# Phase tables of the S5 chunks made on GpSimd instead of VectorE

## The chip, the cores and the metric

The kernel runs on one core of one Trainium2 chip. The metric is the device time of one execution in microseconds (us), the median of three runs: 1687.13 us before the change (1683.44 to 1687.8).

## The reference, cut to what matters

One decoder layer is computed for 1024 prompt tokens and 32 sample tokens (8 sequences of 4), 1056 columns in all. A combined projection `h @ w_in` gives queries, keys, values, the S5 input `u` and gate logits. Branch A is windowed attention. Branch B, the one that matters here, is a diagonal complex recurrence per group of 16 channels (64 groups, 64 states each):

```
dt = exp(log_dt);  decay = exp(lam_re * dt)
ab_re, ab_im = decay * cos(lam_im * dt), decay * sin(lam_im * dt)     # A_bar
h_t = A_bar * h_(t-1) + B_bar * u_t                                   # scan over positions
y_t = Re(C h_t) + D * u_t
```

Then gelu, a GLU projection, a gated merge of both branches, the output projection, RMSNorm, a squared-ReLU MLP and a final RMSNorm.

## The kernel before, in words

All matrix products run in split precision: each float32 factor is cut into a high part (`whi`, cast on ScalarE, L91) and a low part (`wlo`, subtraction on VectorE, L92), and TensorE makes three products of them (L117 to L119). `w_in` is loaded in blocks of 128 columns; `tile_in` (L505) multiplies one block with all 1056 tokens in three chunks of 352. Three PSUM banks (`mm`) take the chunks in turn, so a bank must be emptied before the third chunk after it begins. For a block of `u`, VectorE empties the bank into `Up` (L435, L440, L441); for a block of gates, ScalarE or VectorE copies it into `gt` (L493, L495), which a DMA takes away.

The S5 branch is worked in eight tiles m of eight groups. The positions are cut into 128 chunks of eight tokens. The scan over chunks is made real by taking the rotation of A_bar out: for that the kernel needs the cosine and sine of the phase of every chunk number k from 0 to 127. They come about in steps:

- `s5_params` (L266 on, VectorE) makes dt, the decay, cosine and sine, the powers of A_bar in `TP`, and then, in a chain of nine doublings of eight small instructions each (L374 to L381, 128x32), the phases of the chunk numbers 1, 2, 4, ..., 64. The last seven go into the tile `TE`.
- `s5_phases` (L404) builds from `TE` two small tables `AB`: 16 low and 8 high parts of the chunk number, cosine and sine. It begins with four memsets (L410, L411) and then doubles the tables in seven steps of six products or sums (L420 to L425), of 32, 64, 128 and 256 elements for the low part and 32, 64 and 128 for the high part. Each step needs the step before it (save that the high part begins anew) and one entry of `TE`.
- Two DMAs of the SyncE queue write `AB` to DRAM (L427), and for each tile m a DMA reads its part back as `ab` (L605).
- `s5_e` (L599 on) multiplies low and high parts out to the full tables `EC` and `ES` of tile m (L619 to L621 on VectorE, L625 and L626 on ScalarE), and `s5_x` uses them (first at L652).

GpSimd has little to do in this stretch: per tile m two products of `s5_a` (L555 and L567), whose results VectorE then adds (L556, L568).

The order of the instructions on each engine and each DMA queue is not the order of the lines. A planner in the framework runs through the program once when it is built, with its own estimate of each instruction's time and with the order of the lines as priority, and writes down one fixed order for each engine. On the chip each engine goes through its own list in that order and waits where an input or a buffer is not ready. So the phase steps stand interleaved with the chain L374 to L381 and with other work of VectorE. The buffers `AB[0]`, `AB[1]` and the work tile `aw` lie in a pool of 20 slabs, 16 of which hold the split activations; they come free from tiles of `s5_loads` and `s5_tables` (the last one, for `aw`, after L403).

Of the kernel before, what the change touches and what calls it, by code (L numbers as in the profile page):

```python
# [45 lines left out]
def hybrid_kernel(tc, xt, cache_k, cache_v, h0, norms, w_in, sinks, w_attn_o, lam_re, lam_im, log_dt,  # L46
                  b_ri, b_ir, c_ri, d_cols, w_glu, w_out, w_up, w_down, w_last,
                  y_cols, y_rows, k_prompt, v_prompt, ssm_prompt, k_sample, v_sample, ssm_sample, dbg=None):
    nc = tc.nc
    uid = [0]  # L50

    def new(pool, shape, dt, tag, bufs=None):
        uid[0] += 1
        return pool.tile(list(shape), dt, tag=tag, name=f"{tag}_{uid[0]}", bufs=bufs)
# [211 lines left out]
    def s5_params(pt, lr, li, ldt):  # L266

        V = nc.vector

        def small(tag, w=G, dt=F32):  # L270
            return new(pt, [P, w], dt, tag)

        def exp(out, x, w):
            k, r, p, xc = small(f"ek{w}", w), small(f"er{w}", w), small(f"ep{w}", w), small(f"ex{w}", w)
            i = small(f"ei{w}", w, I32)
            V.tensor_scalar(xc, x, -87.0, 88.0, op0=ALU.max, op1=ALU.min)
            V.tensor_scalar(k, xc, LOG2E, MAGIC, op0=ALU.mult, op1=ALU.add)
            V.tensor_scalar(k, k, -MAGIC, None, op0=ALU.add)
            V.scalar_tensor_tensor(r, k, -LN2_HI, xc, op0=ALU.mult, op1=ALU.add)
            V.scalar_tensor_tensor(r, k, -LN2_LO, r, op0=ALU.mult, op1=ALU.add)  # L280
            V.tensor_scalar(i, k, 8388608.0, 127 * 8388608.0, op0=ALU.mult, op1=ALU.add)
# [122 lines left out]
    def s5_phases(TE):  # L404

        AB = [new(slabA, [P, KT, 24, 4], F32, "slab") for _ in range(2)]
        aw = new(slabA, [P, KT, 2, 8, 4], F32, "slab")
        V = nc.vector
        for o in (0, 16):
            V.memset(AB[0][:, :, o:o + 1], 1.0)  # L410
            V.memset(AB[1][:, :, o:o + 1], 0.0)  # L411
        for i in range(7):
            o, h = (0, 1 << i) if i < 4 else (16, 1 << (i - 4))
            sh = [P, KT, h, 4]
            cb = TE[:, i][:, :, None, :].to_broadcast(sh)
            sb = TE[:, 7 + i][:, :, None, :].to_broadcast(sh)
            x, y = AB[0][:, :, o:o + h], AB[1][:, :, o:o + h]
            zc, zs = AB[0][:, :, o + h:o + 2 * h], AB[1][:, :, o + h:o + 2 * h]
            w1, w2 = aw[:, :, 0, 0:h], aw[:, :, 1, 0:h]
            V.tensor_tensor(zc, x, cb, op=ALU.mult)  # L420
            V.tensor_tensor(w1, y, sb, op=ALU.mult)
            V.tensor_tensor(zs, y, cb, op=ALU.mult)
            V.tensor_tensor(w2, x, sb, op=ALU.mult)
            V.tensor_tensor(zc, zc, w1, op=ALU.subtract)
            V.tensor_tensor(zs, zs, w2, op=ALU.add)  # L425
        for i in range(2):
            nc.sync.dma_start(abdram[:, i], AB[i])  # L427
# [267 lines left out]
    tile_in()  # L695
    us = [s5_u(0)]
    s5_phases(ft[2])
    w2 = s5_a(0)
    tile_in()
# [532 lines left out]
    V = nc.vector  # L1232
# [430 lines left out]
```

## Time and profile before

| | |
|---|---|
| median of the runs | 1687.13 us (1683.44 to 1687.8) |
| the profiled execution, own time | 1690.28 us |
| its span, first to last instruction | 1688.6 us |
| TensorE matmul busy | 1647.2 us, 98% of the span |
| VectorE busy | 1227.5 us, 73% |
| ScalarE busy | 874.6 us, 52% |
| GpSimd busy | 246.6 us, 15%, 229 instructions |
| mean granted TensorE clock | 0.991 of full speed |

The profile comes from one execution. Engines are PE (TensorE matmul), PEld (its weight load), DVE (VectorE), ACT (ScalarE), POOL (GpSimd) and SP (SyncE); a name such as SPq is the engine's queue, which issues DMAs. Times in a timeline count from the start of the span. What an instruction waited for stands in square brackets behind its row: the idle time of its engine, and what ended it. A duration in a timeline includes the time in which an instruction that has been issued waits for a port.

### The profile page before, as it was taken

The page shows a single profiled execution, that of the slowest core. Times are in us where ns is not written, and L with a number is a line of the kernel's source. Part 1 is how long each engine was busy: PE and PEld are TensorE (multiplying, and loading weights), DVE is VectorE, ACT ScalarE, POOL GpSimd, SP SyncE. Part 2 cuts the span into 40 slices and gives each one's busy share as a digit, 9 for nine tenths or more (in the row PEclk, how much of TensorE's full clock was granted, in tenths as well). Part 3 has the DMA queues.
Part 4 walks back from the last instruction along what each step waited for, and adds up shares of the span by engine and source line. Part 5 has one row for each costly group of instructions (what it writes and reads, how often), then busy time and mean ns, then how long its engine had stood idle before and what let it go on. Part 6 is the DMA issues. An engine that isn't in the chain of part 4 may idle for free. (4 is left out here: it accounts for less than half of the span.)

```text
span 1688.6 us, 30936 instructions
## 1 busy us (share of the span) xinstructions
PE 1647.2 (98%) x11976; PEld 1613.3 (96%) x11976; DVE 1227.5 (73%) x2460; ACT 874.6 (52%) x1889; POOL 246.6 (15%) x229
## 2 busy tenths in 40 slices
PE   9999999999999999989999999999999999999998
PEld 8989899999999898989999999999999999999987
DVE  7977888753489999842644677777777788787866
ACT  6234454434567788643433655444444645454544
POOL 1102111101233344320222330000000000000010
PEclk9999999999999999988999999999999999999999
DMA  6334344435502211232343553444444665353422
GB/s 246 113 115 130 106 124 141 136 107 164 206 26 89 78 52 64 84 119 89 123 146 128 187 168 115 153 151 151 150 145 147 224 203 180 109 180 118 123 63 104
DMA packets 133992, 221.84 MB, mean 131 GB/s; under 512 B 14012, under 2 KB 86796, under 8 KB 133332
## 3 DMA queue, kind: packets, MB, share of 16 engines
q1 hardware_dynamic: 86756, 170.81, 31.6%
q10 hardware_dynamic: 45360, 46.63, 8.2%
q0 software_dynamic: 1728, 2.41, 0.5%
q8 instruction: 94, 1.54, 0.4%
q14 instruction: 54, 0.44, 0.1%
HBM read 150.58 MB, written 69.22 MB: 130 GB/s over the span
## 5 line engine op out<-in xcount | busy, mean ns | idle before, releaser
L117 PE MATMUL mm<-slab,whi 128*128 128x352 f32 (+3 forms) x1688 | 535.9, 320 | 8.6 <-DVE Up L440 3.3
L118 PE MATMUL mm<-slab,whi 128*128 128x352 f32 (+3 forms) x1688 | 530.4, 314 | 1.9 <-DVE slab L994 1.9
L119 PE MATMUL mm<-slab,wlo 128*128 128x352 f32 (+3 forms) x1688 | 530.7, 315 | 0.3 <-DVE wlo L92 0.3
L1248 PE MATMUL ax<-slab,w 128*128 128x264 f32 x3600 | 451.6, 285 | 1.8 <-DVE acc L1323 1.8
L1248 PEld LDWEIGHTS ax<-slab,w 128*128 128x128 f32 x3600 | 443.8, 188 | 3.0 <-DVE acc L1323 2.7
L117 PEld LDWEIGHTS mm<-slab,whi 128*128 128x128 f32 x1688 | 320.1, 190 | 12.8 <-PE mm L119 4.4
L118 PEld LDWEIGHTS mm<-slab,whi 128*128 128x128 f32 x1688 | 321.6, 191 | 4.0 <-DVE slab L994 3.3
L119 PEld LDWEIGHTS mm<-slab,wlo 128*128 128x128 f32 x1688 | 320.4, 190 | 1.0 <-DVE wlo L92 0.6
L1248 PE MATMUL mm<-slab,w 128*128 128x264 f32 x1440 | 186.7, 284 | 1.8 <-DVE w L1359 1.1
L1248 PEld LDWEIGHTS mm<-slab,w 128*128 128x128 f32 x1440 | 179.8, 188 | 2.5 <-DVE w L1359 1.3
L91 ACT CAST whi<-raw 128x1024 fp32r<-128x1024 f32 x76 | 79.7, 1049 | 90.2 <-PE mm L118 64.7
L1359 DVE TENSOR_TENSOR w<-raw,w 128x512 fp32r<-128x512 f32 (+2 forms) x96 | 63.0, 657 | 77.1 <-ACT w L1358 73.3
L92 DVE TENSOR_TENSOR wlo<-raw,whi 128x1024 fp32r<-128x1024 f32 x76 | 97.5, 1283 | 22.4 <-ACT whi L91 22.2
L1560 POOL TENSOR_TENSOR slab<-slab,slab 128x512 f32<-128x512 f32 x7 | 9.1, 1294 | 633.1 <-ACT slab L1557 633.1
L1358 ACT CAST w<-whi 128x512 fp32r<-128x512 f32 (+2 forms) x64 | 38.0, 594 | 70.1 <-PE ax L1248 43.4
L839 ACT ACTIVATE pm<-pm,sm 128x128 f32<-128x128 f32 x128 | 49.9, 391 | 34.1 <-DVE sm L836 34.0
L815 POOL TENSOR_TENSOR qs<-q,qs 64x256 fp32r<-64x256 f32 x64 | 58.1, 907 | 63.7 <-ACT qs L814 32.3
L1272 ACT ACTIVATE slab<-slab 128x264 f32<-128x264 f32 x80 | 33.9, 425 | 59.8 <-DVE slab L1271 44.1
L1358 ACT CAST w<-raw 128x512 fp32r<-128x512 f32 (+2 forms) x96 | 56.8, 593 | 9.6 <-PE mm L1248 7.9
L854 POOL TENSOR_TENSOR pt<-fb,pt 128x512 fp32r<-128x512 f32 x28 | 41.7, 1488 | 123.4 <-ACT pt L853 80.1
L567 POOL TENSOR_TENSOR tmp<-bbs,TP 128x1024 f32<-128x1024 f32 x8 | 23.2, 2897 | 209.6 <-DVE W L556 172.9
L1359 DVE TENSOR_TENSOR w<-wlo,w 128x512 fp32r<-128x512 f32 (+2 forms) x64 | 42.1, 658 | 4.8 <-ACT w L1358 3.7
(407 smaller groups left out, 2661.4 us busy)
## 6 DMA issues: line engine op xcount, KB each, us to landing
raw<-in_w_in_dram SPq DMA_DIRECT2D x36, 512.0 KB
raw<-in_w_up_dram SPq DMA_DIRECT2D x32, 512.0 KB
ffd<-slab ACTq DMA_DIRECT2D x28, 528.0 KB
gt<-ffd SPq DMA_DIRECT2D x53, 264.0 KB
slab<-ffd SPq DMA_DIRECT2D x53, 264.0 KB
raw<-in_w_down_dram SPq DMA_DIRECT2D x22, 512.0 KB
gd<-gt ACTq DMA_DIRECT2D x48, 176.0 KB
slab<-gd SPq DMA_DIRECT2D x16, 528.0 KB
```

The source lines that it names most:

```text
L91: nc.scalar.copy(hi[:, :nk], raw[:, :nk])
L92: nc.vector.tensor_tensor(lo[:, :nk], raw[:, :nk], hi[:, :nk].bitcast(F32), op=ALU.subtract)
L117: nc.tensor.matmul(ps[:, :cw], w[0][:, k, :], ah[k][:, cs], start=(k == 0), stop=False)
L118: nc.tensor.matmul(ps[:, :cw], w[0][:, k, :], al[k][:, cs], start=False, stop=False)
L119: nc.tensor.matmul(ps[:, :cw], w[1][:, k, :], ah[k][:, cs], start=False, stop=(k == nk - 1))
L815: nc.gpsimd.tensor_tensor(qs[b, :, h], q[a, :, bs], qs[a, :, h].bitcast(F32), op=ALU.subtract)
L839: nc.scalar.activation(pm[:, i], pm[:, i], AF.Exp, bias=ng[:, i:i + 1], accum_out=den[:, i:i + 1])
L854: lo(pt[:, 1], src, pt[:, 0].bitcast(F32), op=ALU.subtract)
L1248: nc.tensor.matmul(ps[:, :CQ], w[:, wp, js], b[:, bp], start=start and j == k == 0, stop=j == n - 1 and k == 2, skip_group_check=True)
L1272: nc.scalar.activation(dst, dst, AF.Square)
L1358: nc.scalar.copy(t[:, 0], s)
L1359: V.tensor_tensor(t[:, 1], s, t[:, 0].bitcast(F32), op=ALU.subtract)
```

## The change

The name `V` in `s5_phases` is bound to GpSimd. With it the four memsets and the 42 products and sums of the phase tables are issued on GpSimd and no longer on VectorE. The DMAs, the shapes, the arithmetic and all other lines stay.

```
         AB = [new(slabA, [P, KT, 24, 4], F32, "slab") for _ in range(2)]
         aw = new(slabA, [P, KT, 2, 8, 4], F32, "slab")
-        V = nc.vector
+        V = nc.gpsimd
         for o in (0, 16):
             V.memset(AB[0][:, :, o:o + 1], 1.0)
             V.memset(AB[1][:, :, o:o + 1], 0.0)
```

## Rows read from the trace of the kernel before

**Rows 1.** The page's line of busy times, shares and instructions per engine.
```profile
PE 1647.2 (98%) x11976; PEld 1613.3 (96%) x11976; DVE 1227.5 (73%) x2460; ACT 874.6 (52%) x1889; POOL 246.6 (15%) x229
```

**Rows 2.** Busy time by window (window, length, engines, clock, DMA share, GB/s).
```profile
56.00:78.00 22.00, 22.00 (x138) 22.00 (x137) 21.43 (x107) 7.08 (x17) 2.31 (x1) 1.00 0.15 49
78.00:98.00 20.00, 18.58 (x115) 18.07 (x114) 18.25 (x19) 2.28 (x6) 6.49 (x2) 1.00 0.46 145
```

**Rows 3.** Waits of PE from 30 to 140 (total us, times, longest).
```profile
PE mm L117 <- DVE Up L435: 2.1, 2, 1.3
PE mm L117 <- DVE gt L495: 1.0, 1, 1.0
PE mm L117 <- DVE Up L440: 0.6, 1, 0.6
```

**Rows 4.** Waits of PE over the whole span.
```profile
PE mm L117 <- DVE Up L440: 3.3, 4, 1.0
PE mm L117 <- DVE Up L435: 2.4, 3, 1.3
```

**Rows 5.** Timeline of DVE from 56 (start, duration, line, names, shape).
```profile
56.78 0.18 DVE L420 TENSOR_TENSOR slab<-slab,slab 128x32 f32<-128x32 f32 x1
56.88 0.19 DVE L422 TENSOR_TENSOR slab<-slab,slab 128x32 f32<-128x32 f32 x1
...
58.78 0.19 DVE L421 TENSOR_TENSOR slab<-slab,slab 128x32 f32<-128x32 f32 x1
```

**Rows 6.** Timeline of DVE from 74, larger steps of the tables.
```profile
74.11 0.23 DVE L420 TENSOR_TENSOR slab<-slab,slab 128x64 f32<-128x64 f32 x1
...
74.92 0.29 DVE L420 TENSOR_TENSOR slab<-slab,slab 128x128 f32<-128x128 f32 x1
75.12 0.30 DVE L421 TENSOR_TENSOR slab<-slab,slab 128x128 f32<-128x128 f32 x1
```

**Rows 7.** One line's instructions (ns min/median/max, first and last start).
```profile
L1112 POOL TENSOR_TENSOR slab<-slab,slab x32: 749/755/1736, 827.2 to 910.9; 128x264 f32<-128x264 f32 x32
L1009 POOL TENSOR_TENSOR slab<-slab,slab x8: 2417/2462/2486, 557.9 to 807.5; 128x1056 f32<-128x1056 f32 x8
```

**Rows 8.** POOL groups by form (count, busy us, mean ns, idle before).
```profile
L262 POOL TENSOR_TENSOR DD<-m,dcol 128x256 f32<-128x256 f32 x1 | 1.6, 1552 | 16.9 <-DVE acc L188 16.9
...
L261 POOL COPY m<-ident 32x16 f32<-32x16 f32 x4 | 0.8, 189 | 0.1
```

**Rows 9.** Timeline of DVE at 21, when L262 starts at 21.23.
```profile
21.08 1.23 DVE L92 TENSOR_TENSOR wlo<-raw,whi 128x1024 fp32r<-128x1024 f32 x1
```

**Rows 10.** Timeline of all engines from 64.
```profile
64.12 2.31 POOL L555 TENSOR_TENSOR tmp<-xc,TP 128x1152 f32<-128x1152 f32 x1 [41.34 <-ACT xc L237]
...
64.21 2.37 DVE L423 TENSOR_TENSOR slab<-slab,slab 128x128 f32<-128x128 f32 x1
```

**Rows 11.** Timeline of all engines from 77 to 86.
```profile
77.80 0.31 DVE L425 TENSOR_TENSOR slab<-slab,slab 128x128 f32<-128x128 f32 x1
...
79.53 4.23 POOL L567 TENSOR_TENSOR tmp<-bbs,TP 128x1024 f32<-128x1024 f32 x1 [13.09 <-DVE W L556]
...
81.20 3.77 DVE L554 TENSOR_TENSOR W<-XC,TP 128x1152 f32<-128x1152 f32 x1
...
84.90 0.74 DVE L435 TENSOR_TENSOR Up<-mm,rb 128x352 f32<-128x352 f32 x1
...
85.78 0.40 PE L117 MATMUL mm<-slab,whi 128*128 128x352 f32 x1 [0.84 <-DVE Up L435]
```

**Rows 12.** Timeline of the SP queue from 74.
```profile
78.14 0.32 SPq L427 DMA_DIRECT2D abd<-slab  x1
...
83.67 1.26 SPq L605 DMA_DIRECT2D ab<-abd  x2
```

**Rows 13.** Timeline of DVE from 92.
```profile
92.45 1.07 DVE L619 TENSOR_TENSOR ep<-ab 128x512 f32<-128x512 f32 x1
93.42 0.72 DVE L435 TENSOR_TENSOR Up<-mm,rb 128x320 f32<-128x320 f32 x1
```

More of the change, by code (lines that the diff above doesn't have):

```diff
@@ L407, in s5_phases @@
         aw = new(slabA, [P, KT, 2, 8, 4], F32, "slab")
-        V = nc.vector
+        V = nc.gpsimd
         for o in (0, 16):
```

## The prediction

> **What bounds the kernel now.** I read the busy line of the page first. TensorE is busy for 1647.2 of 1688.6 us; all its idle time together is 41.4 us [rows 1]. So VectorE's work counts only where TensorE waits for it, and the second view is the busy time by window around the phase tables. From 56 to 78 us TensorE is busy for 22.00 of 22.00 us and VectorE for 21.43: VectorE is full, but TensorE does not feel it. From 78 to 98 TensorE loses 20.00 - 18.58 = 1.42 us, at the full granted clock (1.00, the 2.4 GHz level) [rows 2]. The third view, the waits of TensorE, names the loss: from 30 to 140 us it waits 2.1 + 1.0 + 0.6 = 3.7 us, each time for VectorE to empty a PSUM bank (L435, L495, L440) [rows 3]. Over the whole span the waits for L440 and L435 are 3.3 + 2.4 us [rows 4]; with the 1.0 for L495 that is 6.7 us, all that a faster VectorE could give back in the projections. The reader is to see in these views that the work which the change moves lies under TensorE's cover, and that the cover ends only some microseconds later, at 84.9: the bank that L435 empties there is one for which TensorE has waited 0.84 us [rows 11].
>
> **What VectorE is rid of.** 42 products and sums: 12 of 32 elements, 12 of 64, 12 of 128, 6 of 256. VectorE's instructions overlap, so the cost is the distance between starts: 56.88 - 56.78 = 0.10 us for 32 elements [rows 5]; (74.92 - 74.11) / 6 = 0.135 for 64, as the six of that step stand in a row; 75.12 - 74.92 = 0.20 for 128 [rows 6]. By the slope of these, about 0.34 for 256 (an estimate). Sum: 12 x (0.10 + 0.135 + 0.20) + 6 x 0.34 = 7.3 us. The four memsets have 32 elements or fewer per row of work and cost at most 4 x 0.10. I take 7.5 us off VectorE. This lies beside a fully busy TensorE, so nothing comes off the span at once; what is late next on VectorE is the L435 at 84.90.
>
> **What GpSimd takes on.** Its row at 264 elements has a median of 0.755 us, the one at 1056 has 2.462 [rows 7]. The line through both has 2.16 ns per element and 0.19 us fixed, thus 0.255, 0.324, 0.462 and 0.74 us for the four sizes, and 12 x (0.255 + 0.324 + 0.462) + 6 x 0.74 = 16.9 us for the 42. The trace shows no product as small as these on GpSimd. From below: the 32x16 copy, 0.189 us, so 42 x 0.189 = 7.9 us. From above: the only product with broadcast operands of this size, 128x256 at 1.552 us [rows 8], 2.1 times the line, so 35.5 us. But that one starts at 21.23 while VectorE's L92 runs from 21.08 to 22.31 [rows 9]; its excess of 0.81 us fits into that collision. I take 16.9. GpSimd is idle for 41.34 us before L555 [rows 10], so its own time is covered, if its results are not late.
>
> **When the tables are ready.** The first step stands at 56.78, the first instruction that needs the work tile at 58.78 [rows 5]. From there 40 more at about 0.4 us each and L555 with 2.31, which stands in the same queue [rows 10]: 58.8 + 16.4 + 2.3 = 77.5, before any collision. The last one now ends at 77.80 + 0.31 = 78.1 [rows 11]. With the waits on GpSimd's side, at most the 12 us or so of other VectorE work in these 20 us (20 less 7.5 of tables), the end lies between 77.5 and 89.5; I take 82. Behind it hang the two stores of the tables and, in order on the same queue, everything SP issues next. The second store is issued at 78.14, the reads that need both at 83.67, that is 5.5 us later [rows 12]; the first instruction that uses what was read starts at 92.45 [rows 13]. Allowing some 2.5 us for the read (an estimate from the 5.5 of a larger store), VectorE has the data at about 86 and reaches L619 6 us after that. Tables that end at 82 are therefore hidden: 4 us later, 6 in hand. On GpSimd the queue behind the tables holds L567 of the first tile and L555 of the second; VectorE's sums and ScalarE's refills of the operands wait for those, but L567 itself waits 13.09 us for VectorE until 79.53 [rows 11], so up to there the tables cost it nothing.
>
> **What comes back to VectorE.** VectorE and GpSimd hinder each other. L423, a 128x128 product that takes 0.30 us elsewhere [rows 6], takes 2.37 when issued 0.09 us after GpSimd's L555, which runs for 2.31 [rows 10]. Later L567 takes 4.23 us, and VectorE's L554, issued in the middle of it, 3.77 [rows 11]. So one of the two stands still while the other reads. Moved tables can therefore cost VectorE the time that they save. Bounds: nothing, if the 42 fall into gaps, so 7.5 us gained; or all of GpSimd's 16.9 us, so 9.4 us lost. To choose, I look at the end of the collision: L423 ends at 66.58 and needs 0.30, so it ran from 66.28, while L555 ended at 66.43 [rows 10]. VectorE was let in 0.15 us before GpSimd's instruction ended, which is about the fixed 0.19 us of the line. So I count only the streaming part: 12 x (32 + 64 + 128) + 6 x 256 = 4224 elements x 2.16 ns = 9.1 us. As the emptying of banks reads PSUM and GpSimd pauses between instructions, I take 85% of it (an estimate): 7.7 us. VectorE: -7.5 + 7.7 = +0.2 us, nothing.
>
> The page "SBUF — State Buffer" of the Trainium skill, section "Who interferes with whom", says that a VectorE instruction with two SBUF inputs and a GpSimd instruction that reads SBUF contend, and that the one that starts first has the shared pair for its whole instruction. This trace agrees in kind (the 2.37 us of L423) and differs by the 0.15 us at the end, which for instructions this short is a third to a half of each; by the page's rule the sum is -7.5 + 16.9 = +9.4 us on VectorE instead of +0.2.
>
> **The sum.** Against the profiled execution (1690.28 us, 1.7 more than its span and 3.2 above the median): off VectorE 7.5, back on it 7.7, and 0.2 us reach the L435 for which TensorE waits. 1690.5 us, or by the distance to the median 1687.3; I say 1687. Its own range, 1684 to 1690.5, is the 3.7 us of waits that may shift when the planner writes new orders around the removed instructions.
>
> **The rivals.** *VectorE really gets free.* If the small instructions of GpSimd fall between those of VectorE, VectorE is 7.5 us ahead at 84.9, and all of the 3.7 us go: 1683.4. If the later waits for banks go too, 6.7 us: 1680.4. For it speaks that an instruction of 32 elements streams for only 0.07 us; against it that VectorE has 0.57 us of gaps in 22 [rows 2].
>
> *The tables come too late* (slower). GpSimd's chain ends past 84 instead of at 82; L619 then stands at the head of VectorE's queue and waits for its operand, and L435, one place behind it [rows 13], keeps a PSUM bank from TensorE. From 84 on each microsecond of the chain is one of TensorE's: at the bound of 89.5, 1687.1 + 5.5 = 1692.6. For it: GpSimd has no priority in a collision that VectorE began (L567, 4.23 us [rows 11]). Against it: the planner may put L619 later.
>
> *GpSimd holds the port for its whole instruction* (slower). VectorE loses 85% of 16.9 = 14.4 us and saves 7.5, net 6.9, and the L435 at 84.9, already 0.84 us late for TensorE, passes that on: 1694.0. It decides from the point where VectorE's loss exceeds the 7.5 us. For it speaks the length of L423; against it the early end just read. That is the time which the rule of the page would give here.
>
> **How the numbers follow.** A change under 0.3%, 5.1 us, is about what a measurement of this kernel cannot tell from none. Forecast 0.50 (0.45 of it within 0.3%, 0.03 below and 0.02 above, for new orders elsewhere); VectorE free 0.25 (0.15 faster by more than 0.3%, the rest not, as 3.7 us is under it); tables late 0.14 (0.11 slower); port held 0.11 (0.09 slower). Sums: faster 0.18, same 0.60, slower 0.22. The range goes down to the full 6.7 us, 1680.4, and up to the port held, 1694; the price of 35.5 us for the chain would lie beyond it.
>
> **What will show it.** Right: VectorE's instructions from 57 to 80 are fewer but several of 0.1 to 0.2 us last 0.3 to 0.6; the 42 on GpSimd sum to some 17 us of undisturbed time, and the last ends between 78 and 84; TensorE's waits for L435, L440 and L495 before 140 stay near 3.7 us. Wrong: these waits gone, or grown past 8 us; a wait of VectorE for the read tables ahead of L619; SP standing at L427 until a weight block is late and ScalarE's L91 waits for a load; a small GpSimd product far from 0.25 to 0.75 us; or a difference that lies in stages after 200 us, which would be a change of order and not of these instructions.

## The result, and the profile after

The changed kernel takes 1697.09 us (median of four runs, 1695.96 to 1699.95); the kernel before, on the same chip, 1685.59 (1683.44 to 1687.8). The ratio is 1.0065, with a 95% interval of 1.0045 to 1.0084: slower by 11.5 us, outside the range of the forecast. All medians in this document are of fast runs: one of the twelve runs of the kernel before that stand beside e1 to e4 took 2655.86 us, at a granted clock of 0.556, and is left out.

The profiled executions are 1696.13 and 1690.28 us. They differ by 5.85 us, less than the medians, since the profiled one of before lies above all its timed runs. So I follow the difference in place. A good mark is the first transpose of S5 on TensorE (L578), which both kernels reach with the same TensorE work behind them: it starts at 124.7 us before and at 133.2 after. Until 75 us the changed kernel is not behind: it has even done 443 matmuls against 436, which is about 1.1 us, as the granted clock until 56 us was 1.00 against 0.97 (six of the twelve kernels from before to e10 show the one and six the other, whichever engine makes the tables). At 120 us it has done 631 against 683. So the 8.5 us have arisen between 75 and 120 us, and this is where to look. (Of these 8.5 us, 2.7 come back between L578 and the end in this pair of executions; I did not follow where.) Each place in time below is read from one execution of its kernel, and the lead at 75 us shows that a difference of about 1 us between two of them can be chance.

The busy line of the page after, to be read against [rows 1]: GpSimd has 46 instructions and 17.4 us more, VectorE 46 fewer but only 3.5 us less, TensorE as much work as before.

```profile
PE 1644.6 (97%) x11976; PEld 1609.9 (95%) x11976; DVE 1224.0 (72%) x2414; ACT 874.4 (52%) x1889; POOL 264.0 (16%) x275
```

Busy time by window after (columns as in [rows 2]: window, length, PE, PEld, DVE, ACT, POOL, granted clock, DMA share, GB/s), first the wide windows, then 4 us each:

```profile
56.00:78.00 22.00, 20.03 (x124) 19.61 (x122) 19.05 (x57) 4.58 (x12) 18.89 (x43) 1.00 0.14 43
78.00:98.00 20.00, 13.18 (x64) 12.92 (x65) 18.25 (x18) 5.34 (x11) 6.51 (x3) 0.83 0.43 138
...
78.00:82.00 4.00, 0.18 (x1) 0.18 (x2) 2.25 (x4) 0.60 (x2) 2.46 (x2) 0.82 0.50 195
82.00:86.00 4.00, 4.00 (x14) 4.00 (x15) 4.00 (x2) 1.66 (x3) 1.78 (x1) 0.50 0.20 46
86.00:90.00 4.00, 4.00 (x23) 4.00 (x22) 4.00 (x6) 0.61 (x2) 2.26 (x1) 0.82 0.02 4
```

TensorE was busy for 18.58 of the 20 us from 78 on in the kernel before; now it is for 13.18. It does next to nothing from 78 to 82, and then the granted clock is 0.50, the 1.2 GHz level, so that 82 to 86 looks full but holds 14 matmuls, where 78 to 82 before, at 1.00, holds 27. The waits of TensorE from 30 to 140 us have grown from 3.7 us [rows 3] to 10.6:

```profile
PE mm L117 <- DVE Up L435: 8.8, 2, 5.8
PE mm L117 <- DVE gt L495: 1.3, 2, 0.7
PE mm L117 <- DVE Up L440: 0.5, 1, 0.5
```

The longest of them stands in TensorE's list as

```profile
81.82 0.66 PE L117 MATMUL mm<-slab,whi 128*128 128x352 f32 x1 [5.79 <-DVE Up L435]
```

VectorE before, the rows to compare with:

```profile
71.92 0.81 DVE L435 TENSOR_TENSOR Up<-mm,rb 128x352 f32<-128x352 f32 x1
72.55 0.21 DVE L381 TENSOR_TENSOR slab<-ha,hr 128x32 f32<-128x32 f32 x1
...
75.73 0.76 DVE L435 TENSOR_TENSOR Up<-mm,rb 128x320 f32<-128x320 f32 x1
...
78.00 1.38 DVE L556 TENSOR_TENSOR W<-W,tmp 128x1152 f32<-128x1152 f32 x1
```

VectorE from 72 us after (start, duration, line, in brackets the idle time before it):

```profile
72.07 0.18 DVE L381 TENSOR_TENSOR slab<-ha,hr 128x32 f32<-128x32 f32 x1
72.17 1.34 DVE L554 TENSOR_TENSOR W<-XC,TP 128x1152 f32<-128x1152 f32 x1
73.44 2.22 DVE L566 TENSOR_TENSOR tmp<-BB,TP 128x1024 f32<-128x1024 f32 x1
79.75 1.36 DVE L556 TENSOR_TENSOR W<-W,tmp 128x1152 f32<-128x1152 f32 x1 [4.08 <-POOL tmp L555]
81.03 0.74 DVE L435 TENSOR_TENSOR Up<-mm,rb 128x352 f32<-128x352 f32 x1
81.63 3.37 DVE L554 TENSOR_TENSOR W<-XC,TP 128x1152 f32<-128x1152 f32 x1
...
84.92 1.21 DVE L568 TENSOR_TENSOR tmp<-tmp,tmp 128x1024 f32<-128x1024 f32 x1
86.05 0.71 DVE L435 TENSOR_TENSOR Up<-mm,rb 128x320 f32<-128x320 f32 x1
```

And GpSimd, the last of the tables and what follows:

```profile
72.29 1.50 POOL L420 TENSOR_TENSOR slab<-slab,slab 128x128 f32<-128x128 f32 x1 [0.19 <-DVE slab L381]
73.75 2.20 POOL L421 TENSOR_TENSOR slab<-slab,slab 128x128 f32<-128x128 f32 x1
...
77.07 0.45 POOL L425 TENSOR_TENSOR slab<-slab,slab 128x128 f32<-128x128 f32 x1
77.48 2.24 POOL L555 TENSOR_TENSOR tmp<-xc,TP 128x1152 f32<-128x1152 f32 x1
81.25 2.53 POOL L567 TENSOR_TENSOR tmp<-bbs,TP 128x1024 f32<-128x1024 f32 x1 [1.54 <-DVE W L556]
```

Three things are to be seen. First, L555 of the first tile, which ran at 64.12 before [rows 10], now stands behind all 42 products and starts at 77.48; VectorE's L556 waits 4.08 us for it. The two engines hold each other up here: the L420 and L421 at 72.29 and 73.75, beside VectorE's L554 and L566, take 1.50 and 2.20 us instead of 0.42, and L555 comes that much later. Second, VectorE's list has another order. Before, L556 and L566 of the first tile stood behind the three evacuations of the first u block; after, L554, L566 and L556 stand ahead of the second one, the L554 of the second tile and L568 ahead of the third. So the second L435 of the block comes at 81.03, and TensorE, which wants the bank, waits 5.79 us. Third, VectorE has hardly gained in the stretch where the tables went: its chain of doublings (L374 to L381) ends with the L381 at 72.07; before it ended with one at 72.55, with one L435 more done by then.

### The profile page after: what moved, and what is told of

It reads as the page before. It is cut to its first block, busy times and chain, and to the rows that moved or that the text cites. A ratio compares the mean times of both kernels' runs of the same rounds, so it can differ in the third digit from the quotient of the medians.

```text
span 1694.4 us, 30947 instructions
## 1 busy us (share of the span) xinstructions
PE 1644.6 (97%) x11976; PEld 1609.9 (95%) x11976; DVE 1224.0 (72%) x2414; ACT 874.4 (52%) x1889; POOL 264.0 (16%) x275
## 5 line engine op out<-in xcount | busy, mean ns | idle before, releaser
L92 DVE TENSOR_TENSOR wlo<-raw,whi 128x1024 fp32r<-128x1024 f32 x76 | 98.0, 1290 | 20.6 <-ACT whi L91 20.3
L567 POOL TENSOR_TENSOR tmp<-bbs,TP 128x1024 f32<-128x1024 f32 x8 | 21.5, 2685 | 208.2 <-DVE W L556 162.4
```

Source lines behind the costliest of these rows:

```text
L92: nc.vector.tensor_tensor(lo[:, :nk], raw[:, :nk], hi[:, :nk].bitcast(F32), op=ALU.subtract)
```

## The experiments

"Before" is in each case the kernel before on the same chip; the first L578 is read from the profile of each kernel (where lines are shifted, the same instruction; e11 and e12 have it elsewhere in TensorE's list). The medians are of 6 to 12 executions each, of four in the first row. The profiled execution can lie some us beside the median: 1678.13 us in e6, 1697.11 in e10, 1683.52 in e12.

| kernel | us, median | before | ratio, 95% interval | first L578 |
|---|---|---|---|---|
| after | 1697.09 | 1685.59 | 1.0065 (1.0045 to 1.0084) | 133.2 (before 124.7) |
| e1_l555_dve | 1696.62 | 1687.97 | 1.0047 (1.0029 to 1.0065) | 133.1 |
| e2_hold | 1694.69 | 1687.97 | 1.0038 (1.0023 to 1.0054) | 130.2 |
| e3_q_first | 1697.28 | 1687.97 | 1.0058 (1.0040 to 1.0076) | 133.2 |
| e4_low_pool | 1697.24 | 1687.97 | 1.0052 (1.0036 to 1.0068) | 134.7 |
| e5_order | 1690.96 | 1688.50 | 1.0017 (1.0003 to 1.0031) | 126.7 |
| e6_noprod_order | 1683.48 | 1688.50 | 0.9968 (0.9954 to 0.9983) | 120.4 |
| e7_noprod | 1689.88 | 1688.50 | 1.0013 (1.0002 to 1.0024) | 128.8 |
| e8_afirst | 1690.47 | 1688.50 | 1.0016 (1.0002 to 1.0031) | 125.5 |
| e9_late_dve | 1689.07 | 1689.28 | 1.0004 (0.9991 to 1.0016) | 118.6 |
| e10_late_u0 | 1693.63 | 1689.28 | 1.0026 (1.0012 to 1.0040) | 123.4 |
| e11_late_b | 1691.17 | 1686.37 | 1.0030 (1.0013 to 1.0046) | other order |
| e12_late_b_hold | 1689.78 | 1686.37 | 1.0018 (1.0003 to 1.0033) | other order |

### Is it the one wait of L556?

The first theory was that the 4.08 us of L556 are the whole loss. Three kernels take that wait away in different ways (e1, e3, e4); in a fourth (e2) it stays, but behind the evacuations of the block.

e1_l555_dve, the product that L556 waits for on VectorE:

```
-        gp.tensor_tensor(tw, ov(xc2, 9), pw(AI0, 9), op=ALU.mult)
+        (gp if m else V).tensor_tensor(tw, ov(xc2, 9), pw(AI0, 9), op=ALU.mult)
```

> The changed kernel, but the product L555 of tile 0 alone is made on VectorE, so VectorE's sum L556 no longer waits for GpSimd's queue; the 42 table products stay on GpSimd with all their collisions. Queue theory (the loss is L556 of tile 0 waiting 4.1 us for L555, which stands behind the 42 products, with a bank evacuation L435 behind it): TensorE's idle time of 5.8 us at 76 to 82 goes, its waits for L435, L495 and L440 from 30 to 140 us fall from 10.6 to 3 to 6 us, no half clock near 82 to 88; time about that of the kernel before, 1685 to 1690, though VectorE does 1.3 us more. Port theory (the loss is VectorE slowed by collisions with the 42 products): nothing of it goes, 1694 to 1698.

e2_hold, L556 of the first tile queued behind the evacuations of the u block (`issue_after` adds an edge to the planner's order, no semaphore):

```
-        V.tensor_tensor(W2, W2, tw, op=ALU.add)
+        with tc.issue_after(first['u'].ins):
+            V.tensor_tensor(W2, W2, tw, op=ALU.add)
```

> The changed kernel, but VectorE's sum L556 of tile 0 is queued on VectorE behind the three bank evacuations (L435) of the u block before it. GpSimd's queue, the collisions and L555's place behind the 42 products stay. Queue theory: L556 starts at about 80 as in the changed kernel, but no evacuation stands behind it, so TensorE's 5.8 us of idle time go; 1685 to 1690. Port theory: 1694 to 1698.

e3_q_first, the tables queued behind that L555 on GpSimd:

```
-    s5_phases(ft[2])
     w2 = s5_a(0)
+    with tc.issue_after(first['a'].ins):
+        s5_phases(ft[2])
```

> The changed kernel, but on GpSimd the 42 table products are queued behind L555 of tile 0 (issued at about 64). Queue theory: L556 finds its operand at 66 to 67 and does not wait; the 5.8 us go; the tables end about 7 us later, at 84 to 86, and the first instruction that uses them (L619) may now be what VectorE waits for, for 0 to 4 us; 1686 to 1692. Port theory: 1694 to 1698.

e4_low_pool, only the four steps of the low table on GpSimd:

```
         for i in range(7):
+            V = nc.gpsimd if i < 4 else nc.vector
```

> Half of the change: only the 24 products of the low table on GpSimd, the 18 of the high table on VectorE. L555 then stands behind 24 products and can start at about 68 instead of 77.5. Queue theory: L556 no longer waits, and the 5.8 us go; 1685 to 1689. Port theory: the collisions are 24 of 42 with 3072 of 4224 elements, so about 6 to 8 of the 11.5 us stay: 1691 to 1694.

All four stay slower by 0.4 to 0.6%, so the theory fell; e1 to e3 lie in the range that was given for the port theory (VectorE slowed by the collisions alone), e4 above it. What TensorE waits for from 30 to 140 us changes its name and keeps its size: 9.6 us in e1, 9.0 in e2, 10.6 in e3, 9.4 in e4. In e2 the L556 is behind the first block, and one wait of 7.09 us stands at the second (L436 is L435 there):

```profile
77.80 0.43 PE L117 MATMUL mm<-slab,whi 128*128 128x352 f32 x1 [1.86 <-DVE Up L436]
92.89 0.63 PE L117 MATMUL mm<-slab,whi 128*128 128x352 f32 x1 [7.09 <-DVE Up L436]
```

In e1 the next waits of VectorE take over (it idles 2.86 us before L568, for L567 of GpSimd), and in e3 they are 4.80 us for L567 and 6.49 for the L555 of the second tile, which stand among the tables and behind them there. What I took from it is that the planner had put more S5 work ahead of the evacuations than this one sum; the next four kernels test that.

### The order held, and the tables taken out

e5_order keeps the change, and queues VectorE's S5 instructions of the first tiles behind the same evacuations as in the kernel before; `ue` holds the evacuations in order, `late(k, ...)` is an `issue_after` on one of them for tile 0, 1. The list that results is not quite that of before: the L554 of the second tile is not held and runs right behind the first one, ahead of the third L435 (before it came at 81.20 [rows 11]), and L556 has come ahead of L441 and L92:

```
+        with late(1): V.tensor_tensor(W2, ov(XC[:, gs], 9), pw(AR0, 9), op=ALU.mult)
+        with late(3, 5): V.tensor_tensor(W2, W2, tw, op=ALU.add)
+        with late(3, 5): V.tensor_tensor(V1, ov1(BB[:, gs]), pv1(AR0), op=ALU.mult)
+        with late(4): V.tensor_tensor(V1, V1, tv, op=ALU.add)
...
```

> The changed kernel (tables on GpSimd), with VectorE's instructions of s5_a and s5_e(0) queued behind the same evacuations of the two u blocks as in the kernel before, so that VectorE's list is that of before less the 42 products (two neighbours change places). Order theory (the time went to S5 products that the planner put ahead of the bank evacuations, because VectorE's list was shorter): within 0.3% of before, or a little below, 1681 to 1690 us; PE's waits on L435 and L440 in 30 to 140 us back to at most 4 us together and no granted clock of 0.5 between 78 and 98. GpSimd theory (the late L555 and L567, and collisions with GpSimd, cost it in any order): 1693 to 1698 us, PE again idle for over 5 us somewhere between 75 and 100.

e6_noprod_order is e5 without the products; e7_noprod is the changed kernel without them, in the planner's own order:

```
-        for i in range(7):
...
+        V.memset(AB[0], 1.0)
+        V.memset(AB[1], 0.0)
```

> Leaves out the 42 products of the tables altogether (two memsets fill them), and keeps VectorE's list in the order of the kernel before, as e5. Neither engine pays for tables. Both theories: 1680 to 1685 us. What lies between this and e5 is what the tables on GpSimd still cost when the order is held; order theory: under 3 us, GpSimd theory: 8 us or more.

> Leaves out the 42 products of the tables altogether (two memsets fill them), and lets the planner order VectorE's list, which it does much as in the changed kernel: the S5 products of the first two tiles and the phases of s5_e(0) stand ahead of the evacuations. Order theory: it loses against before though nobody makes the tables, 1690 to 1697 us, with PE idle for 5 us or more on L435 or L440 between 75 and 100 (the line numbers of this kernel are kept). GpSimd theory: 1680 to 1685 us, since GpSimd is free for L555 and L567 and nothing collides with 42 products.

e8_afirst is the kernel before with two lines exchanged:

```
-    s5_phases(ft[2])
     w2 = s5_a(0)
+    s5_phases(ft[2])
```

> The kernel before (tables on VectorE), with s5_a(0) written ahead of s5_phases, so that L554, L566 and L556 of the first tile stand ahead of the third L435 of the first u block, as in the changed kernel, with GpSimd's list otherwise as before. Order theory: VectorE comes late to the evacuations, 1690 to 1697 us with PE waits on L435 of over 6 us in 30 to 140. GpSimd theory: within 0.3% of before.

With the order held, most of the loss is gone: e5 is 2.5 us above before instead of 11.5, and the first L578 comes 6.5 us earlier than after. No granted clock of 0.5 is left between 78 and 98 us, and the waits for L435 and L440 are 3.5 us together, as the order theory gave; its 1690 us are missed by 0.96, and the 1693 of the other by more. e6 lies in the range that both theories gave. But the distance from e5 to it, 7.5 us of time, is not the "under 3" of the order theory and nearly the "8 or more" of the GpSimd theory: the tables do cost on GpSimd, though hardly more than on VectorE. Between e5 and e6, which have the same list but for the products, the 6.3 us at L578 can be followed row by row. VectorE in e5:

```profile
72.05 0.18 DVE L381 TENSOR_TENSOR slab<-ha,hr 128x32 f32<-128x32 f32 x1
...
72.80 2.97 DVE L554 TENSOR_TENSOR W<-XC,TP 128x1152 f32<-128x1152 f32 x2
75.70 0.75 DVE L435 TENSOR_TENSOR Up<-mm,rb 128x320 f32<-128x320 f32 x1
76.28 0.23 DVE L440 TENSOR_TENSOR Up<-mm,rb 128x32 f32<-128x32 f32 x1
79.15 1.36 DVE L556 TENSOR_TENSOR W<-W,tmp 128x1152 f32<-128x1152 f32 x1 [2.65 <-POOL tmp L555]
...
86.07 0.74 DVE L435 TENSOR_TENSOR Up<-mm,rb 128x352 f32<-128x352 f32 x1
```

and in e6:

```profile
68.59 0.19 DVE L381 TENSOR_TENSOR slab<-ha,hr 128x32 f32<-128x32 f32 x1
...
72.24 0.76 DVE L435 TENSOR_TENSOR Up<-mm,rb 128x320 f32<-128x320 f32 x1 [0.29 <-PE mm L119]
72.83 0.23 DVE L440 TENSOR_TENSOR Up<-mm,rb 128x32 f32<-128x32 f32 x1
72.91 1.35 DVE L556 TENSOR_TENSOR W<-W,tmp 128x1152 f32<-128x1152 f32 x1
...
79.69 0.80 DVE L435 TENSOR_TENSOR Up<-mm,rb 128x352 f32<-128x352 f32 x1
```

The chain ends 3.46 us later beside GpSimd's products, and the third L435 comes as much later. Then 2.65 us go to the wait for L555, and from there the lists run in parallel, 6.38 us apart at the next L435. So with the order held the tables cost 6.3 us on GpSimd and, from 124.7 - 120.4, 4.3 us on VectorE: moving them costs 2.0 (2.5 by the medians, with an interval from 0.03 to 0.31%). The other 6.5 of the 8.5 us are gone when the list is held.

e7 shows that a list of the planner's can lose by itself. Nobody makes the tables there, and still L578 comes 8.4 us later than in e6; S5 work up to s5_e(0) stands ahead of the evacuations (the changed kernel has no L619 or L620 ahead of the third L435, e7 has), and TensorE waits

```profile
PE mm L117 <- ACT slab L626: 4.3, 1, 4.3
PE mm L117 <- DVE Up L440: 2.0, 1, 2.0
```

The name L626 is probably not the cause: the evacuation and the matmul that waits are

```profile
90.67 1.33 DVE L435 TENSOR_TENSOR Up<-mm,rb 128x352 f32<-128x352 f32 x2
91.55 0.63 PE L117 MATMUL mm<-slab,whi 128*128 128x352 f32 x1 [4.28 <-ACT slab L626]
```

and the 0.88 us between their starts are the same as in e5 (86.07 to 86.95) and before (84.90 to 85.78), where L435 is named.

The time of e7 (+1.4 us against before) undershot the 1690 to 1697 us that the order theory gave, by 0.12 us. e8 does not decide between the theories: 1690.47 us lies in the range of the one and within the 0.3% of the other. TensorE does wait 5.8 us on L435, but the interval reaches down to 0.02%, and L578 is 0.8 us late. There the stall is made good, since TensorE then works 22.00 of the 22 us from 98 to 120, where before it worked 19.65. Nor is its list that of the changed kernel: L554, L566 and L556 stand ahead of the third evacuation, not of the second. So the order of e8 alone is not worth 6.5 us. That the planner's list costs as much in the changed kernel because GpSimd's results, for which the advanced sums wait, are late too, is argued and not shown: I did not separate these two any further.

### Can the 5 us of e6 be had?

If the tables cost only because they stand ahead of evacuations, they should be free later. e9_late_dve puts them back on VectorE, and queues the first product of the first step behind the L440 of the second u block; the others follow it because they need its result or the work tile, but for two that run at 65.46 and 65.66. The S5 sums of `s5_a` are held as in e5. e10_late_u0 does it with the first block.

```
+            with (tc.issue_after(ue[7].ins) if i == 0 else nullcontext()): V.tensor_tensor(zc, x, cb, op=ALU.mult)
```

> The kernel before, tables on VectorE, with the first product of each of the seven sizes queued behind the L440 of the second u block (most of the 42 products then run there, at about 89 to 100 us), and the S5 instructions of the first two tiles held behind the evacuations as in e5. If the account of e5 and e6 holds (what the tables cost is VectorE's time between 56 and 94 us, ahead of evacuations, whoever makes them; from 98 to 140 VectorE has some 13 us without work in e6 and before), the evacuations come as early as in e6: first L578 at 120 to 123 us, PE waits of 30 to 140 us under 3 us, 1682 to 1687 us, below both kernels. Rival: the phases are wanted early (through the copies L625 and L626 in ScalarE's queue, ahead of the weights' casts), so that the later tables give the wait to PE between 100 and 130 us, 1690 to 1697 us.

> As e9, with the products queued behind the L440 of the first u block instead (at about 73 us), so that most of them stand among the evacuations of the second u block. By the account of e5 and e6 they are back on the path there: about as before, 1685 to 1691 us, first L578 at 124 to 126 us. By the rival of e9 it is better than e9, since the tables are earlier.

The first half came true: in e9 no wait for a bank is left from 30 to 140 us, and L578 comes at 118.6. But the rival was right on the second half. The wait has moved to the copies of `W1`, in the S5 products:

```profile
PE ax L648 <- ACT W L580: 6.8, 2, 4.0
```

ScalarE's list shows why. The second L580 stands behind the issue of a gate's DMA (L496), which waits for an L495 of VectorE (127.63), late behind phase products (L619 to L621):

```profile
122.32 0.58 ACT L580 COPY W<-ax 128x512 f32<-128x512 f32 x1
128.19 0.33 ACTq L496 DMA_DIRECT2D gd<-gt  x1
128.56 0.58 ACT L580 COPY W<-ax 128x512 f32<-128x512 f32 x1 [5.66 <-DVE gt L495]
```

From 120 to 140 us the granted clock is then 0.74, and by the end nothing is left of the 6 us: 1.0004. The time, 1689.07 us, lies between the two ranges on record. e10, with the same wait and evacuations among the tables, is slower, 1693.63 us; neither account had foreseen that. Two more moves of the source aim at that list.

e11_late_b is e9 with s5_b(0) written ahead of the fifth tile, and e12_late_b_hold holds the phases of the second tile as well:

```
     es_ = s5_e(0)
-    tile_in()
     w13 = s5_b(0, *w2)
+    tile_in()
```

> e9, and s5_b(0) written ahead of the fifth tile_in instead of behind it, so that in ScalarE's list the two copies L580 of the first tile stand together, ahead of the tile's DMAs L496 (in e9 one L496, waiting for a late L495, stood between them and held L648 for 4.0 of its 6.8 us). If e9's remaining loss is that order, L648 waits for under 3 us, 1682 to 1686 us, below both kernels. Rival: the products on VectorE cost their time wherever they stand, and the wait moves on to another of its readers, 1687 to 1692 us.

> e11, and the first products of the second tile's phases (L619 of s5_e(1)) queued behind the L440 of the third u block, so that the prefetched phases stand less in the way of the evacuations between 100 and 125 us. If VectorE's list there is what remains, 1 to 3 us below e11; if not, within 0.1% of e11.

e11 misses its range and lies in that of its rival. e12 lies 1.4 us below e11, which is both "1 to 3 us below" and within 0.1%, so it decides nothing. The wait for L580 is gone from e11, but TensorE now works 15.67 of the 20 us from 120 to 140 and 16.41 of the next 20, in many short stops (L495 2.2, L435 2.2, L440 1.8 us by 160). They are 0.3 and 0.2% slower than before. No version found here beats the kernel before; only leaving the products out does.

## Why the prediction was wrong

- **The cost of the 42 on GpSimd** was right. The line gave 0.255, 0.324, 0.462 and 0.74 us; undisturbed they take 0.25, 0.31, 0.42 to 0.47 and 0.64 to 0.75. GpSimd's busy time rises by 17.4 us, with four memsets and the collisions in it, and with an L567 that is 1.7 us shorter than before (2.53 against 4.23); the sum was 16.9.
- **The end of the tables** was forecast too late, and its lower bound was met by luck: the last product ends at 77.5, where 77.5 to 89.5 was the range and 82 was taken. The 77.5 had L555 with its 2.3 us ahead of the end, but it ran behind the tables, and collisions (the 1.50 and 2.20 us above, and 1.25 for a product of 0.25) made up for it. L619 never waited for its operand, so the rival of late tables is out.
- **The balance of VectorE**, "+0.2 us", came out near the mark, in part by luck. With the order held (e5) the third L435 of the first u block comes at 75.70 against 75.73 before, though one L554 more stands ahead of it. The first L435 of the next block has the same other work ahead of it in both lists; it is 1.17 us late (86.07 against 84.90), and that includes 2.65 us of waiting for L555. Both terms were too large. The removal brings 5.2 us at this row (79.69 in e6), not 7.5. The collisions of the products take 5.5 us from the chain, not 7.7: the 3.46 us between e5 and e6, and 2.1 that e6 pays in a collision of L555 with one L374 (2.25 us instead of 0.18) and e5 does not. The kernel before pays as much at L423 [rows 10]; that this falls away with the move stood in neither term.
- **The step that failed** is the sentence on GpSimd's queue: "On GpSimd the queue behind the tables holds L567 of the first tile and L555 of the second ... so up to there the tables cost it nothing." It holds L555 of the first tile too, which moved from 64.12 to 77.48. That instruction was even in the sum for the end of the tables, 2.3 us, but its own reader L556 was not asked. With the order held this is a wait of 2.65 us in front of the next evacuations; the next L435 comes 1.17 us later than before, and L578 2.0.
- **What was put far too low** is the larger part, 6.5 of 8.5 us: that VectorE's list would be written anew. "Its own range" allowed 3.7 us for new orders, in waits that were there already, and so at most 3.5 us more than before. In fact the new list has sums that depend on GpSimd ahead of evacuations that TensorE depends on, and TensorE waits 10.6 us; with the list held (e5) most of that is gone. The idle time then cost a second time, at the half clock from 82 on: 14 matmuls in 4 us where 27 fit is about 2 us. Why the planner chose this list is not shown, and how much of the 6.5 us is order alone stays open (e8).
- **The rival of the held port** came nearest in time, 1694.0, but by luck: its loss of VectorE of 6.9 us net is not to be seen in e5. The own mark for "wrong", waits grown past 8 us, was met: 10.6.

## What to carry to other kernels

Work moved to an idle engine is queued there in front of something; list every instruction behind it, and for each one ask who reads it and what stands behind that reader. Where a planner writes the order, removing instructions from an engine's list can move the rest of it too, and here this cost more than the work was worth: hold the order with edges once, to see which of the two a result is, and compare the list that comes out with the one that was meant. A wait that goes away in one list comes back in the next (e1 to e4, e9 to e12), so read a gain at the end of the span and not at the wait.

## What the hardware showed

Two small streams on VectorE and GpSimd ran in lockstep. Both engines in the changed kernel, from 65 us:

```profile
65.21 0.64 POOL L422 TENSOR_TENSOR slab<-slab,slab 128x256 f32<-128x256 f32 x1
65.34 0.56 DVE L379 SCALAR_TENSOR_TENSOR ha<-slab 128x32 f32<-128x32 f32 x1
65.80 0.64 POOL L423 TENSOR_TENSOR slab<-slab,slab 128x256 f32<-128x256 f32 x1
65.82 0.67 DVE L380 TENSOR_TENSOR slab<-hb,hr 128x32 f32<-128x32 f32 x1
66.39 0.75 POOL L424 TENSOR_TENSOR slab<-slab,slab 128x256 f32<-128x256 f32 x1
66.41 0.77 DVE L381 TENSOR_TENSOR slab<-ha,hr 128x32 f32<-128x32 f32 x1
67.08 0.75 POOL L425 TENSOR_TENSOR slab<-slab,slab 128x256 f32<-128x256 f32 x1
67.11 1.80 DVE L92 TENSOR_TENSOR wlo<-raw,whi 128x1024 fp32r<-128x1024 f32 x1
67.78 1.25 POOL L420 TENSOR_TENSOR slab<-slab,slab 128x32 f32<-128x32 f32 x1
```

Each of VectorE's 32-element instructions, 0.18 us elsewhere, lasts as long as the GpSimd instruction beside it, 0.56 to 0.77 us, and GpSimd keeps its undisturbed 0.64 to 0.75. At the end it is the other way about: L92 has begun, and a GpSimd product of 0.25 us takes 1.25. So in these rows the one that has begun holds the other up, in both directions. In kind this agrees with the rule of the Trainium skill, "SBUF — State Buffer", section "Who interferes with whom", that the one that issues first blocks the other for its whole instruction. The end reads as in the prediction, where it was 0.15 us: L380 ends at 66.49 and needs 0.18, so it ran from 66.31, 0.13 us before the L423 beside it ended at 66.44; the same working gives 0.13 to 0.14 for L379, L381, L92 (1.22 us alone in e6) and, on GpSimd, the L420. Whether the port is handed over early, or the recorded end of an instruction lies behind its last access, no run here separates.

So the price of a collision was forecast well, and its share was not: 5.5 us of toll are 60% of the 9.1 us of streaming, where 85% was taken (an estimate from the chain of e5 and e6). A toll is paid only while both engines have work: the products lay 8.6 us without a gap on GpSimd (59.2 to 67.8), and of these VectorE lost 3.9 (the L381 that starts at 66.39 in e5 starts at 62.46 in e6).
